# A hybrid decoder layer on one core: places of the splits and norms at the feed-forwards' ends, keys turned in three places, and the third output's place in the mixer

## The chip, the cores and the metric

The kernel runs on one core of one Trainium2 chip. The core has TensorE (matmul, PE in the profile, with its weight loads PEld), VectorE (DVE), ScalarE (ACT), GpSimd (POOL) and SyncE (SP), each with its own queue, and 16 DMA engines. The metric is the device time of one execution in microseconds.

## The reference, cut to what matters

One decoder layer over 512 tokens of 1024 features, all in float32:

```
h = x + 1/2 * swiglu_1(rmsnorm(x))                    # d_ff 2816
z = rmsnorm(h) @ w_in                                 # columns split among two groups of heads
    attention: window 128, 8 query heads on 2 key/value heads of 64, norm of q and k, rotary, sinks
    gated linear attention: 4 heads, keys of 64, values of 128, decay per key dimension, in chunks
    gla = rmsnorm(gla) * silu(gate)
h = h + concat(attention, gla) @ w_out
h = h + 1/2 * swiglu_2(rmsnorm(h))
h = h + sigmoid(rmsnorm(h) @ ple_w_gate) * rmsnorm(p @ ple_w_proj)
```

## The kernel before

The 512 tokens are four tiles of 128. Every large product is done in three matmuls: an operand is split into a rounded part ("hi") and the rest ("lo"), and hi x hi, hi x lo and lo x hi are added up in PSUM (`mm3`). Activations come out of PSUM by a cast on ScalarE (hi) and a subtraction on VectorE (lo) in `split_psum`. Weights are loaded by SP into two raw buffers (`wraw`), and `Weights.split` casts each on ScalarE (`whi`, L140) and subtracts on VectorE (`wlo`, L141) into a ring of five slots. `W.get(key, ahead)` traces the splits up to that unit and `ahead` units beyond; `stops` bounds how far.

The program's stages follow each other: the first feed-forward, the embedding's product (`pe`), the mixer's projections with both attentions, the output projection (`wo`), the second feed-forward, and the gate's product (`pgt`).

A planner orders the instructions of each engine: it simulates the program and takes what is ready by its own costs and urgencies, so the order of the text is not the order of the queues. Two things bind it. `on_pe` puts TensorE's instructions of a step behind the last one traced, which fixes TensorE's order in the mixer. `in_order` does so for TensorE, ScalarE and VectorE, for a list of steps. SP's and POOL's queues aren't bound by either.

At the end of a feed-forward, `last_tiles` lists by hand: `pd(t, q)` (six matmuls of the last down product of tile t), `update(t)` (two additions into h on VectorE, L391), `squares(t)` (ScalarE, L307), `factor(t)` (a small addition on VectorE and a power on POOL, L299), `scaled(t)` (VectorE, L316) and `turned(t)` (eight transposes of tile t on TensorE, L202, and the casts and subtractions out of PSUM). Tiles 0 and 1 are turned in the list, tiles 2 and 3 by the code that follows: behind the second and third tile of the embedding's product, and ahead of the second and third tile of the gate's. `keep(t)` saves a tile of h to memory from SP's queue. `split_gates` splits the first unit of the gate's weights.

In the mixer one list gives TensorE's order. Its PSUM has three groups of two: `psA`, `psG` (one bank each) and `psD` (two banks each). `turn_decay` turns the decayed keys (`kd`) of three token tiles one after the other through `psG`, and ScalarE copies each out (L893). `gla_decays(li)` makes the decays of level li: two subtractions (L823, L824), an exponential (L825) and two multiplications (L826, L827) in a tile `X`. `X`, `kd` and the two score matrices `At` share a tag of four slots. `gla_level(li)` multiplies them on TensorE (`gr`), and VectorE merges the result (L854). `gla_diagonal` (`gd`) is the level of single tokens. `gla_out(c)` is the output of token tile c in a `psD` bank pair: a square on ScalarE, a sum and a scale on VectorE (L927, L928), a power on POOL, and a multiplication out of PSUM (L932) that frees the pair. `attention_out` splits the attention's half (L955, L956), `gla_mix` multiplies by the gate (L943) and turns, `out_half` is the first half of the output projection for two tiles.

Of the kernel before, what the change touches and what calls it, by code (L numbers as in the profile page):

```python
# [152 lines left out]
def hymba_kernel(tc, A, out):  # L153
# [33 lines left out]
    def psG(name):  # L187
        return psp.tile([P, 512], F32, name=name, tag="psG", bufs=2)
# [12 lines left out]
    def turn(o, x):  # L201
        last_pe[0] = nc.tensor.transpose(o, x, idn).ins  # L202

    def on_pe(f, *args):

        with tc.issue_after(last_pe[0]):
            return f(*args)
# [74 lines left out]
    add_ffn(2)  # L282
    W.stops.insert(2, len(W.units))
    for c0 in (0, 512):
        for k0 in (0, 4):
            W.add_rows("pg", A["ple_w_gate"], k0, 4, c0, 512)


    last_pow = [None]
# [31 lines left out]
        norm_scaled(t, gain, nrm, norm_factor(t, name, ss))  # L321
        return t, nrm, nT, name

    def last_tiles(pd, update, gain, nT, name, third=(), fourth=()):


        sq, rs = {}, {}

        def squares(t):
            sq[t] = norm_squares(t, name)  # L330

        def factor(t):
            rs[t] = norm_factor(t, name, sq[t][1])

        def scaled(t):
            norm_scaled(t, gain(), sq[t][0], rs[t])

        def turned(t):
            norm_transpose(t, sq[t][0], nT, name, (psA, psG))

        in_order((pd, 0, 0), (pd, 1, 0), (pd, 0, 1), (update, 0), (squares, 0), (pd, 1, 1), (update, 1), (factor, 0),
                 (squares, 1), (pd, 2, 0), (pd, 2, 1), *third, (scaled, 0), (update, 2), (factor, 1), (squares, 2),
                 (pd, 3, 0), (pd, 3, 1), (scaled, 1), *fourth, (turned, 0), (update, 3), (factor, 2), (squares, 3),
                 (scaled, 2), (turned, 1), (factor, 3), (scaled, 3))
        return turned

    def norm_transpose(t, nrm, nT, name, bank=(psG, psG)):
# [209 lines left out]
    with tc.tile_pool(name="ffn1p", bufs=1, reuse_waits="tile") as fp:  # L557
        gm = gain_tile("mix_norm")
        nTm = norm_pair(xp, "mix")
        h_d = [drp.tile([P, D], F32, name=f"h_d{t}") for t in range(NT)]  # L560

        turned = []

        def finish1(pd, update):
            turned.append(last_tiles(pd, update, lambda: gm, nTm, "mx", (), [(keep, 0), (keep, 1), (keep, 2)]))
            keep(3)

        def keep(t):
            nc.sync.dma_start(out=h_d[t], in_=h[t])

        ffn(1, nT1, fp, finish1, fp, fp, None, 2)
# [39 lines left out]
    for t in range(0, NT, 2):  # L611
        eo = mp.tile([P, 8, 256], F32, name=f"eo{t}", tag="e", bufs=2).rearrange("p (t a) c -> p t (a c)", t=2)
        for i in range(2):
            ps = psD(f"pe{t + i}")
            for c in range(2):
                gemm_ts(ps[:, c], pT, t + i, [wpe[c]])
            nc.scalar.copy(eo[:, i], ps.rearrange("p a c -> p (a c)"))
            nc.sync.dma_start(out=emb_d[t + i], in_=eo[:, i])
            if t + i in (1, 2):
                turned[0](t + i + 1)  # L620


    kall = t2("kall")
# [260 lines left out]
        nc.vector.tensor_mul(kd, kd, kF)  # L884
        Xs["k"] = kdC

    def turn_decay():
        kdC = Xs.pop("k")
        for c in range(3):
            ps = psG(f"kdt{c}")  # L890
            for a in range(2):
                turn(ps[:, a * P:(a + 1) * P], kdC[:, a * 4 + c, :])
            nc.scalar.copy(kdT[:, c], ps[:, :256].rearrange("p (a c) -> p a c", a=2))  # L893

    def gla_state(c):
        dS = psG(f"dS{c}").rearrange("p (a c) -> p a c", c=P)
# [74 lines left out]
    for f, *args in (  # L971
            (queries, 0), (turn_ranks,), (queries, 1), (turn_keys,), (log_decays, 0), (queries, 2), (log_decays, 1),
            (queries, 3), (sums, 0), (turn_queries, 0), (gla_qk, 0), (sums, 1), (turn_queries, 1), (scores, 0),
            (gla_qk, 1), (turn_queries, 2), (scores, 1), (gla_qk, 2), (turn_queries, 3), (turn_scores, 0, 0),
            (gla_qk, 3), (gla_decay,), (gla_decays, 0), (scores, 2),
            (gla_v, 0), (weighted, 0), (turn_decay,), (gla_diagonal,), (turn_scores, 1, 0), (gla_decays, 1),
            (gla_v, 1), (gla_level, 0), (gla_state, 0), (turn_scores, 1, 1), (gla_decays, 2),
            (gla_v, 2), (gla_level, 1), (weighted, 1), (gla_state, 1), (scores, 3), (gla_decays, 3),
            (gla_v, 3), (gla_level, 2), (gla_state, 2), (turn_scores, 2, 0), (gla_decays, 4),
            (gla_gate, 0), (gla_level, 3), (turn_scores, 2, 1), (gla_decays, 5),  # L980
            (gla_gate, 1), (gla_level, 4), (weighted, 2), (turn_scores, 3, 0), (gla_decays, 6),
            (gla_gate, 2, 0), (gla_level, 5), (turn_scores, 3, 1), (gla_gate, 2, 1), (gla_level, 6), (gla_scores_out,),
            (weighted, 3), (gla_gate, 3, 0), (gla_out, 0), (gla_silu, 0), (gla_out, 1), (gla_silu, 1),
            (gla_gate, 3, 1), (gla_silu, 2), (gla_silu, 3), (attention_out,), (gla_out, 2),
            (gla_mix, 0, mixT), (gla_out, 3), (gla_mix, 1, mixT), (out_half, 0, 0), (out_half, 0, 1),
            (gla_mix, 2, mixT), (out_half, 1, 0), (out_half, 1, 1),
            (gla_mix, 3, mixT)):
        on_pe(f, *args)
# [9 lines left out]
    with tc.tile_pool(name="ffn2p", bufs=1, reuse_waits="tile") as fp:  # L998
# [36 lines left out]
            g3.append(gain_tile("ple_gate_norm"))  # L1035

        nT3 = norm_pair(np_, "pg")
        def split_gates():
            W.get(("pg", 0, 0), 0)

        def finish2(pd, update):
            turned[:] = [last_tiles(pd, update, lambda: g3[0], nT3, "pg", [(split_gates,)])]

        ffn(2, nT2, fp, finish2, xp, xp, "nhi", 2, lambda: norm_transpose(*pend2[NT - 1]), embedding_norm)

# [1 line left out]
    with tc.tile_pool(name="outp", bufs=1, reuse_waits="tile") as op:  # L1047
        emb = []
        for t in range(NT):
            e = op.tile([P, D], F32, name=f"emb{t}")  # L1050
            with tc.issue_after(last_pow[0]):
                nc.gpsimd.dma_start(out=e, in_=emb_d[t])
            emb.append(e)
        for c0 in (0, 512):
            tiles = [W.get(("pg", c0, k)) for k in (0, 2, 4, 6)]
            for t in range(NT):
                if c0 == 0 and t in (1, 2):
                    turned[0](t + 1)
                parts = ((0, 256), (256, 512)) if c0 and t == NT - 1 else ((0, 512),)
                for a, b in parts:  # L1060
                    sl = slice(c0 + a, c0 + b)
                    ps = psA(f"pgt{c0}_{t}_{a}")[:, :b - a]
                    gemm_ts(ps, nT3, t, [(wh[:, :, a:b], wl[:, :, a:b]) for wh, wl in tiles])
                    sg = op.tile([P, 512], F32, name=f"sgm{c0}_{t}_{a}", tag="sgm", bufs=3)[:, :b - a]
                    nc.scalar.activation(sg, ps, AF.Sigmoid)
                    nc.vector.tensor_mul(sg, sg, emb[t][:, sl])
                    nc.vector.tensor_add(sg, sg, h[t][:, sl])
                    nc.sync.dma_start(out=out[t * P:(t + 1) * P, sl], in_=sg)
# [59 lines left out]
```

## Time and profile before

| | |
|---|---|
| median of 3 runs | 1008.62 us (1008.01 to 1010.85) |
| the profiled execution | 1008.22 us |
| its span | 1006.5 us |
| TensorE matmuls busy | 971.2 us (96%) |
| TensorE weight loads busy | 807.4 us (80%) |
| VectorE busy | 645.0 us (64%) |
| ScalarE busy | 394.5 us (39%) |
| GpSimd busy | 43.7 us (4%) |
| mean granted TensorE clock | 0.989 |
| DMA | 109.91 MB, mean 109 GB/s |

The span is the time from the first to the last instruction of the profiled execution; the device time is a little longer. Busy shares are means over the whole span. A busy TensorE can still run at half clock, which the granted clock of a stretch shows.

### The profile page before, as it was taken

Reading aid. Unit: us, or ns where it says so; the run is one execution under the profiler, and the core shown is the slowest. Engines: PE = TensorE matmul, PEld = TensorE weight load, DVE = VectorE, ACT = ScalarE, POOL = GpSimd, SP = SyncE. Lnnn points to the kernel's source line nnn. Section 1 sums busy time; section 2 is a strip of 40 time slices with the busy share of each in tenths; the row PEclk is TensorE's granted clock in tenths of the full one; section 3 lists DMA queues with packets and bytes.
Section 4 is the critical chain, followed back from the end, with each engine's and each line's share of the span. In section 5 each row is a group of like instructions: output and inputs, shape, how many; then the busy total and the mean of one; then the engine's idle time right before and its main releaser. Section 6 shows DMA issues by size and latency. Waiting matters only on the chain.

```text
span 1006.5 us, 12373 instructions
## 1 busy us (share of the span) xinstructions
PE 971.2 (96%) x5090; PEld 807.4 (80%) x5090; DVE 645.0 (64%) x811; ACT 394.5 (39%) x569; POOL 43.7 (4%) x55
## 2 busy tenths in 40 slices
PE   5999999999999989998998999999999999999898
PEld 5988888888888879876766789888888888888687
DVE  6567667576675764775766364766677675757652
ACT  5443333333333245585455243333344333332441
POOL 4000000000000010200002010000000000000010
PEclk9999999999999999999998999999999999999999
DMA  8715133141330255220213246142252523303231
GB/s 290 250 47 168 41 126 125 46 167 40 126 105 1 88 186 184 88 85 1 58 50 98 84 163 242 42 168 84 96 205 75 169 83 106 124 1 104 74 126 53
DMA packets 74235, 109.91 MB, mean 109 GB/s; under 512 B 5937, under 2 KB 55234, under 8 KB 74178
## 3 DMA queue, kind: packets, MB, share of 16 engines
q1 hardware_dynamic: 72450, 102.82, 30.4%
q0 software_dynamic: 1728, 6.29, 1.8%
q8 instruction: 40, 0.66, 0.2%
q14 instruction: 17, 0.14, 0.0%
HBM read 100.72 MB, written 8.39 MB: 108 GB/s over the span
## 4 chain that ended last, share of the span: by engine, by line
PE 88%; DVE 6%; ACT 2%; DMA 2%; issue 1%; POOL 0%; SPq 0%; ACTq 0%; POOLq 0%; DVEq 0%
PE pg L199 24%; PE pu L199 24%; PE pd L199 20%; PE pgt L199 5%; PE wo L199 4%; PE aq L199 2%; PE pe L199 1%; PE kvr L199 1%; PE gqk L199 1%; PE gv L199 1%; PE gog L199 1%; DVE mx L724 1%; DMA wraw<-in_w_out_dram 1%; DVE wlo L141 1%; DVE e L722 1%
## 5 line engine op out<-in xcount | busy, mean ns | idle before, releaser
L140 ACT CAST whi<-wraw 128x1024 fp32r<-128x1024 f32 (+1 forms) x126 | 129.9, 1039 | 187.4 <-PE pd L199 136.3
L141 DVE TENSOR_TENSOR wlo<-wraw,whi 128x1024 fp32r<-128x1024 f32 (+1 forms) x124 | 149.9, 1215 | 56.0 <-ACT whi L140 53.7
L199 PE MATMUL pg<-nlo_f,whi 128*128 128x512 f32 (+1 forms) x384 | 143.0, 373 | 0.0
L199 PE MATMUL pg<-nhi_f,whi 128*128 128x512 f32 (+1 forms) x384 | 142.6, 373 | 0.2 <-ACT nhi_f L292 0.2
L199 PE MATMUL pu<-nhi_f,wlo 128*128 128x512 f32 (+1 forms) x384 | 142.6, 372 | 0.0
L199 PE MATMUL pg<-nhi_f,wlo 128*128 128x512 f32 (+1 forms) x384 | 142.6, 372 | 0.0
L199 PE MATMUL pu<-nlo_f,whi 128*128 128x512 f32 (+1 forms) x384 | 142.6, 372 | 0.0
L199 PE MATMUL pu<-nhi_f,whi 128*128 128x512 f32 (+1 forms) x384 | 142.4, 372 | 0.0
L199 PE MATMUL pd<-whi,ahi 128*128 128x512 f32 x312 | 121.4, 389 | 0.0
L199 PE MATMUL pd<-wlo,ahi 128*128 128x512 f32 x312 | 121.4, 389 | 0.0
L199 PE MATMUL pd<-whi,alo 128*128 128x512 f32 x312 | 120.6, 389 | 0.0
L391 DVE SCALAR_TENSOR_TENSOR h<-pd,h 128x512 f32<-128x512 f32 x116 | 76.5, 686 | 29.5 <-PE pd L199 29.5
L199 PEld LDWEIGHTS pg<-nhi_f,whi 128*128 128x128 f32 x384 | 72.3, 189 | 13.2 <-ACT nhi_f L292 0.7
L199 PEld LDWEIGHTS pg<-nlo_f,whi 128*128 128x128 f32 x384 | 72.6, 189 | 12.9 <-DVE nlo_f L293 0.6
L199 PEld LDWEIGHTS pg<-nhi_f,wlo 128*128 128x128 f32 x384 | 72.5, 189 | 12.5
L199 PEld LDWEIGHTS pu<-nhi_f,wlo 128*128 128x128 f32 x384 | 72.3, 188 | 12.5
L199 PEld LDWEIGHTS pu<-nhi_f,whi 128*128 128x128 f32 x384 | 72.2, 188 | 12.5
L199 PEld LDWEIGHTS pu<-nlo_f,whi 128*128 128x128 f32 x384 | 72.4, 188 | 12.3
L140 ACT CAST whi<-draw 128x1024 fp32r<-128x1024 f32 x35 | 36.8, 1053 | 96.9 <-PE pu L199 50.9
L431 DVE TENSOR_TENSOR cb<-pu,sg 128x512 f32<-128x512 f32 x44 | 30.3, 690 | 69.2 <-PE pu L199 69.2
L140 ACT CAST whi<-wpr 128x1024 fp32r<-128x1024 f32 x35 | 36.9, 1053 | 96.2 <-PE pu L199 58.2
L199 PEld LDWEIGHTS pd<-whi,ahi 128*128 128x128 f32 x312 | 58.6, 188 | 12.2
(243 smaller groups left out, 1466.5 us busy)
## 6 DMA issues: line engine op xcount, KB each, us to landing
wraw<-in_ffn_w_gate_dram SPq DMA_DIRECT2D x22, 1024.0 KB, 5.0
wraw<-in_ffn_w_up_dram SPq DMA_DIRECT2D x22, 1024.0 KB, 5.0
wpr<-in_ffn_w_down_dram SPq DMA_DIRECT2D x10, 1024.0 KB, 5.6
draw<-in_ffn_w_down_dram SPq DMA_DIRECT2D x10, 1024.0 KB, 5.2
wraw<-in_w_in_dram SPq DMA_DIRECT2D x8, 1024.0 KB, 4.9
wraw<-in_ple_w_gate_dram SPq DMA_DIRECT2D x4, 1024.0 KB, 4.8
h<-in_x_dram SPq DMA_DIRECT2D x4, 512.0 KB, 7.0
wraw<-in_ffn_w_down_dram SPq DMA_DIRECT2D x4, 512.0 KB, 3.4
```

The lines of the kernel that those rows point to most:

```text
L140: nc.scalar.copy(hi, v)
L141: (nc.gpsimd if u < 2 and i else nc.vector).tensor_tensor(lo, v, hi.bitcast(F32), op=ALU.subtract)
L199: last_pe[0] = nc.tensor.matmul(o, lhsT=l, rhs=r, start=start, stop=stop_, **kw).ins
L391: nc.vector.scalar_tensor_tensor(hs, x, 0.5, hs, ALU.mult, ALU.add)
L431: nc.vector.tensor_mul(cb[:, half].rearrange("p a c -> p (a c)"), pu, sg)
L722: nc.vector.tensor_add(half, sc[:, :, :, :nk], amask[:, 256 - nk:].unsqueeze(1).unsqueeze(1).broadcast_to([P, 2, 2, nk]))
L724: nc.vector.reduce_max(mxt.rearrange("p (g a) -> p g a", g=2)[:, :, 2 * a:2 * a + 2], half, AX.X)
```

## The change

The gate's first 512 columns are split into weight units of two, two and four row blocks instead of four and four. `last_tiles` gets a new common part and, from its callers, a list of places for what follows the last products; tiles 2 and 3 of the first feed-forward are turned one embedding tile earlier; those of the second within the gate product, behind its first half, and that product is bound to the traced order in halves. In the mixer the three turns of the decayed keys are separate steps, copied out by VectorE, the diagonal goes ahead of them, and the fourth scores go ahead of the second state; the third output follows the second half of the fourth gate directly, ahead of the SiLUs and the attention's split, and the fourth output ahead of the first mix.

```diff
@@ -282,8 +282,8 @@
     add_ffn(2)
     W.stops.insert(2, len(W.units))
     for c0 in (0, 512):
-        for k0 in (0, 4):
-            W.add_rows("pg", A["ple_w_gate"], k0, 4, c0, 512)
+        for k0, nk in ((0, 2), (2, 2), (4, 4)) if c0 == 0 else ((0, 4), (4, 4)):
+            W.add_rows("pg", A["ple_w_gate"], k0, nk, c0, 512)
 
 
     last_pow = [None]
@@ -321,7 +321,7 @@
         norm_scaled(t, gain, nrm, norm_factor(t, name, ss))
         return t, nrm, nT, name
 
-    def last_tiles(pd, update, gain, nT, name, third=(), fourth=()):
+    def last_tiles(pd, update, gain, nT, name, places):
 
 
         sq, rs = {}, {}
@@ -338,10 +338,10 @@
         def turned(t):
             norm_transpose(t, sq[t][0], nT, name, (psA, psG))
 
-        in_order((pd, 0, 0), (pd, 1, 0), (pd, 0, 1), (update, 0), (squares, 0), (pd, 1, 1), (update, 1), (factor, 0),
-                 (squares, 1), (pd, 2, 0), (pd, 2, 1), *third, (scaled, 0), (update, 2), (factor, 1), (squares, 2),
-                 (pd, 3, 0), (pd, 3, 1), (scaled, 1), *fourth, (turned, 0), (update, 3), (factor, 2), (squares, 3),
-                 (scaled, 2), (turned, 1), (factor, 3), (scaled, 3))
+        named = {"pd": pd, "update": update, "squares": squares, "factor": factor, "scaled": scaled, "turned": turned}
+        in_order((pd, 0, 0), (pd, 1, 0), (pd, 0, 1), (update, 0), (squares, 0), (pd, 1, 1), (update, 1), (squares, 1),
+                 (factor, 0), (pd, 2, 0), (pd, 2, 1), (scaled, 0), (factor, 1), (update, 2), (scaled, 1),
+                 (pd, 3, 0), (pd, 3, 1), *((named.get(f, f), *args) for f, *args in places))
         return turned
 
     def norm_transpose(t, nrm, nT, name, bank=(psG, psG)):
@@ -562,8 +562,10 @@
         turned = []
 
         def finish1(pd, update):
-            turned.append(last_tiles(pd, update, lambda: gm, nTm, "mx", (), [(keep, 0), (keep, 1), (keep, 2)]))
-            keep(3)
+            turned.append(last_tiles(pd, update, lambda: gm, nTm, "mx", [
+                ("update", 3), ("turned", 0), ("squares", 2), ("factor", 2), ("turned", 1), ("squares", 3),
+                (keep, 0), (keep, 1), ("scaled", 2), ("factor", 3), (keep, 2), (lambda: W.get(("kvr", 0, 0), 0),),
+                ("scaled", 3), (keep, 3)]))
 
         def keep(t):
             nc.sync.dma_start(out=h_d[t], in_=h[t])
@@ -616,8 +618,8 @@
                 gemm_ts(ps[:, c], pT, t + i, [wpe[c]])
             nc.scalar.copy(eo[:, i], ps.rearrange("p a c -> p (a c)"))
             nc.sync.dma_start(out=emb_d[t + i], in_=eo[:, i])
-            if t + i in (1, 2):
-                turned[0](t + i + 1)
+            if t + i < 2:
+                turned[0](t + i + 2)
 
 
     kall = t2("kall")
@@ -884,13 +886,12 @@
         nc.vector.tensor_mul(kd, kd, kF)
         Xs["k"] = kdC
 
-    def turn_decay():
-        kdC = Xs.pop("k")
-        for c in range(3):
-            ps = psG(f"kdt{c}")
-            for a in range(2):
-                turn(ps[:, a * P:(a + 1) * P], kdC[:, a * 4 + c, :])
-            nc.scalar.copy(kdT[:, c], ps[:, :256].rearrange("p (a c) -> p a c", a=2))
+    def turn_decay(c):
+        kdC = Xs["k"]
+        ps = psG(f"kdt{c}")
+        for a in range(2):
+            turn(ps[:, a * P:(a + 1) * P], kdC[:, a * 4 + c, :])
+        nc.vector.tensor_copy(kdT[:, c], ps[:, :256].rearrange("p (a c) -> p a c", a=2))
 
     def gla_state(c):
         dS = psG(f"dS{c}").rearrange("p (a c) -> p a c", c=P)
@@ -973,16 +974,16 @@
             (queries, 3), (sums, 0), (turn_queries, 0), (gla_qk, 0), (sums, 1), (turn_queries, 1), (scores, 0),
             (gla_qk, 1), (turn_queries, 2), (scores, 1), (gla_qk, 2), (turn_queries, 3), (turn_scores, 0, 0),
             (gla_qk, 3), (gla_decay,), (gla_decays, 0), (scores, 2),
-            (gla_v, 0), (weighted, 0), (turn_decay,), (gla_diagonal,), (turn_scores, 1, 0), (gla_decays, 1),
-            (gla_v, 1), (gla_level, 0), (gla_state, 0), (turn_scores, 1, 1), (gla_decays, 2),
-            (gla_v, 2), (gla_level, 1), (weighted, 1), (gla_state, 1), (scores, 3), (gla_decays, 3),
+            (gla_v, 0), (weighted, 0), (gla_diagonal,), (turn_decay, 0), (turn_scores, 1, 0), (gla_decays, 1),
+            (gla_v, 1), (gla_level, 0), (turn_decay, 1), (gla_state, 0), (turn_scores, 1, 1), (gla_decays, 2),
+            (gla_v, 2), (gla_level, 1), (weighted, 1), (turn_decay, 2), (scores, 3), (gla_state, 1), (gla_decays, 3),
             (gla_v, 3), (gla_level, 2), (gla_state, 2), (turn_scores, 2, 0), (gla_decays, 4),
             (gla_gate, 0), (gla_level, 3), (turn_scores, 2, 1), (gla_decays, 5),
             (gla_gate, 1), (gla_level, 4), (weighted, 2), (turn_scores, 3, 0), (gla_decays, 6),
             (gla_gate, 2, 0), (gla_level, 5), (turn_scores, 3, 1), (gla_gate, 2, 1), (gla_level, 6), (gla_scores_out,),
-            (weighted, 3), (gla_gate, 3, 0), (gla_out, 0), (gla_silu, 0), (gla_out, 1), (gla_silu, 1),
-            (gla_gate, 3, 1), (gla_silu, 2), (gla_silu, 3), (attention_out,), (gla_out, 2),
-            (gla_mix, 0, mixT), (gla_out, 3), (gla_mix, 1, mixT), (out_half, 0, 0), (out_half, 0, 1),
+            (weighted, 3), (gla_gate, 3, 0), (gla_out, 0), (gla_out, 1), (gla_gate, 3, 1), (gla_out, 2),
+            (gla_silu, 0), (gla_silu, 1), (attention_out,), (gla_out, 3), (gla_silu, 2), (gla_silu, 3),
+            (gla_mix, 0, mixT), (gla_mix, 1, mixT), (out_half, 0, 0), (out_half, 0, 1),
             (gla_mix, 2, mixT), (out_half, 1, 0), (out_half, 1, 1),
             (gla_mix, 3, mixT)):
         on_pe(f, *args)
@@ -1035,11 +1036,14 @@
             g3.append(gain_tile("ple_gate_norm"))
 
         nT3 = norm_pair(np_, "pg")
-        def split_gates():
-            W.get(("pg", 0, 0), 0)
+        def split_gates(k):
+            W.get(("pg", 0, k), 0)
 
         def finish2(pd, update):
-            turned[:] = [last_tiles(pd, update, lambda: g3[0], nT3, "pg", [(split_gates,)])]
+            split_gates(0)
+            turned[:] = [last_tiles(pd, update, lambda: g3[0], nT3, "pg", [
+                ("squares", 2), ("turned", 0), ("factor", 2), (split_gates, 2), (split_gates, 4), ("turned", 1),
+                ("scaled", 2), ("update", 3), ("squares", 3), ("factor", 3), ("scaled", 3)])]
 
         ffn(2, nT2, fp, finish2, xp, xp, "nhi", 2, lambda: norm_transpose(*pend2[NT - 1]), embedding_norm)
 
@@ -1054,13 +1058,18 @@
         for c0 in (0, 512):
             tiles = [W.get(("pg", c0, k)) for k in (0, 2, 4, 6)]
             for t in range(NT):
-                if c0 == 0 and t in (1, 2):
-                    turned[0](t + 1)
                 parts = ((0, 256), (256, 512)) if c0 and t == NT - 1 else ((0, 512),)
                 for a, b in parts:
                     sl = slice(c0 + a, c0 + b)
                     ps = psA(f"pgt{c0}_{t}_{a}")[:, :b - a]
-                    gemm_ts(ps, nT3, t, [(wh[:, :, a:b], wl[:, :, a:b]) for wh, wl in tiles])
+                    wt = [(wh[:, :, a:b], wl[:, :, a:b]) for wh, wl in tiles]
+                    if c0 == 0:
+                        on_pe(gemm_ts, ps, nT3, t, wt[:2], False)
+                        if t in (1, 2):
+                            on_pe(turned[0], t + 1)
+                        on_pe(gemm_ts, ps, nT3, t, wt[2:], True, 4)
+                    else:
+                        gemm_ts(ps, nT3, t, wt)
                     sg = op.tile([P, 512], F32, name=f"sgm{c0}_{t}_{a}", tag="sgm", bufs=3)[:, :b - a]
                     nc.scalar.activation(sg, ps, AF.Sigmoid)
                     nc.vector.tensor_mul(sg, sg, emb[t][:, sl])
```

## Rows read from the trace of the kernel before

**Rows 1.** The page: busy time (share of the span) and instructions of an engine.
```profile
PE 971.2 (96%) x5090; PEld 807.4 (80%) x5090; DVE 645.0 (64%) x811; ACT 394.5 (39%) x569; POOL 43.7 (4%) x55
```
**Rows 2.** TensorE's waits: line, for what, total us, times, longest us.
```profile
PE kdt L202 <- ACT kdT L893: 3.9, 1, 3.9
PE o L199 <- DVE on L932: 3.7, 2, 3.5
PE ntr_pg L202 <- ACT whi L140: 3.7, 1, 3.7
PE pe L199 <- DVE h L391: 2.5, 1, 2.5
...
PE ntr_pg L202 <- DVE nrm_pg L316: 1.0, 1, 1.0
```
**Rows 3.** Windows: length, busy PE, PEld, DVE, ACT, POOL, granted clock, DMA, GB/s.
```profile
370.40:373.80 3.40, 3.40 (x10) 2.63 (x9) 2.67 (x5) 0.67 (x2) 1.25 (x4) 0.50 0.57 227
373.80:465.90 92.10, 86.57 (x476) 71.33 (x474) 59.97 (x99) 55.88 (x122) 10.50 (x8) 1.00 0.31 103
466.00:469.40 3.40, 3.40 (x71) 2.95 (x72) 2.49 (x4) 2.95 (x7) 0.00 (x0) 0.50 0.00 0
506.90:510.30 3.40, 3.40 (x10) 2.63 (x9) 3.40 (x5) 1.92 (x5) 0.00 (x0) 0.50 0.00 0
544.50:551.30 6.80, 6.80 (x26) 5.42 (x27) 4.30 (x9) 1.19 (x2) 2.30 (x3) 0.50 0.00 0
954.10:957.50 3.40, 3.40 (x12) 2.92 (x11) 3.02 (x6) 2.06 (x6) 1.37 (x1) 0.50 0.79 301
```
**Rows 4.** Timeline of TensorE, 368 to 380: start, us, what [idle before <- releaser].
```profile
369.14 0.50 PE L199 MATMUL pe<-whi,pTwhi 128*128 128x512 f32 x1 [2.51 <-DVE h L391]
...
376.36 1.91 PE L202 MATMUL ntr_mx<-idn,nrm_mx 128*128 128x128 f32 x16
```
**Rows 5.** Timeline of VectorE, 363 to 371.
```profile
365.34 1.35 DVE L141 TENSOR_TENSOR wlo<-wraw,whi 128x544 fp32r<-128x544 f32 x2
366.61 1.28 DVE L293 TENSOR_TENSOR nlo_mix<-ntr_mx,nhi_mix 128x512 fp32r<-128x512 f32 x2
367.81 1.28 DVE L391 SCALAR_TENSOR_TENSOR h<-pd,h 128x512 f32<-128x512 f32 x2
```
**Rows 6.** The chain that ended last, in the mixer: start, us, what.
```profile
466.62 1.92 PE gd L199 x64
...
478.13 5.47 PE gv L199 x24
```
**Rows 7.** Timeline of ScalarE, 461 to 470.
```profile
465.52 0.62 ACT L893 COPY kdT<-kdt 128x256 f32<-128x256 f32 x2
```
**Rows 8.** Timeline of VectorE, 460 to 512: decays, and copies of the first state.
```profile
476.57 0.69 DVE L823 TENSOR_TENSOR X<-bT 128x512 f32<-128x512 f32 x1 [4.40 <-PE gr L199]
...
477.78 0.48 DVE L905 COPY S<-dS 128x128 f32<-128x128 f32 x2
...
479.91 0.68 DVE L827 TENSOR_TENSOR X<-X,gqT 128x512 f32<-128x512 f32 x1
...
498.91 0.68 DVE L823 TENSOR_TENSOR X<-bT 128x512 f32<-128x512 f32 x1
...
508.03 0.69 DVE L827 TENSOR_TENSOR X<-X,gqT 128x512 f32<-128x512 f32 x1
```
**Rows 9.** Timeline of VectorE, 538 to 547.
```profile
540.19 1.89 DVE L956 TENSOR_TENSOR nlo_mo<-araw,nhi_mo 128x512 fp32r<-128x512 f32 x3
...
543.65 0.69 DVE L932 TENSOR_TENSOR on<-o,rs_o 128x512 f32<-128x512 f32 x1 [0.30 <-POOL rs_o L299]
```
**Rows 10.** Timeline of VectorE, 944 to 958.
```profile
949.98 2.35 DVE L141 TENSOR_TENSOR wlo<-wraw,whi 128x1024 fp32r<-128x1024 f32 x2
952.25 1.28 DVE L316 SCALAR_TENSOR_TENSOR nrm_pg<-h,rs_pg,gain_ple_gate_norm 128x1024 f32<-128x1024 f32 x1
```
**Rows 11.** DMA issues: out<-in, queue, count, KB each, median us to landing.
```profile
wraw<-in_ple_w_gate_dram SPq DMA_DIRECT2D x4, 1024.0 KB, 4.8
```

## The prediction

> **What bounds the kernel now.** I read the page first, then TensorE's own waits, then the granted clock, and at last the order of the instructions round the few places that these two point to. The page shows the kernel bound by TensorE: its matmuls are busy for 971.2 of 1006.5 us [rows 1]. So only what TensorE loses counts, and that is little: some 35 us in the whole span, part of it at the start. The list of its waits names single places [rows 2]: 2.5 us ahead of the embedding's product at the end of the first feed-forward, 3.9 us in the transposes of the decayed keys, 3.7 us at the outputs, and 1.0 and 3.7 us in the transposes at the end of the second feed-forward. The stretches of rows 3 are what follows such a wait: the granted clock is 0.50, the 1.2 GHz level, for 3.4 us, once for 6.8 us, and 1.00 (2.4 GHz) for the 92 us between the first and the second of them. An engine busy throughout at half clock does in 3.4 us the work of 1.7, so each stretch costs up to 1.7 us on top of the wait ahead of it. The change touches four of the five stretches of rows 3; the one at 506.9 it leaves alone.
>
> **Base.** The profiled execution took 1008.2 us, 1.7 around its span of 1006.5; the median of the runs is 0.4 above it. I subtract from 1008.2.
>
> **1. End of the first feed-forward.** The embedding's product waits for tile 3's residual update, which frees the PSUM banks it will use: idle 2.51 us until 369.14 [rows 4]. On VectorE that update starts at 367.81, though its product was done at about 364.5 (an estimate: 369.14 less the 2.51 us and less some 2 us for the 16 transposes ahead, which take 1.91 us elsewhere in rows 4). Ahead of it on VectorE went two key-weight subtractions of 1.35 us together, which the planner had pulled in from later code, and a pair of 1.28 us for the first transposes [rows 5]. The new list puts the update first, so it ends near 366.0, before the transposes of tiles 0 and 1 do. The wait goes (2.5), and with it the half clock that follows (up to 1.7). What is late next is tile 2's norm: VectorE now does update, two pairs of subtractions and the scaling, four pieces of 1.28 us [rows 5] from 364.7, with some 0.6 us of waits on ScalarE, so it is ready at about 370.5. Tile 2's transposes are now traced behind the first embedding tile instead of the second, that is at 364.5 + 1.9 + 2.7 (half of a 24-matmul product, 5.47 us [rows 6]) = 369.1. The cost is 0 if the planner lets the second tile pass, 1.4 if it doesn't; I take 0.6, since before it swapped such transposes with products too. Term 1: 2.5 + 1.7 - 0.6 = **3.6**, ends 2.8 and 4.2; a loss is out, since nothing new is put ahead of the embedding's product.
> Other queues: the four saves of h on SP move behind the squares; they are read only after the mixer. The key weights' split moves some 5 us later, and with it the next load into its raw buffer; that weight is multiplied more than 20 us later, behind the embedding and the keys, and without that cover the load would cost up to the 5 us.
>
> **2. Keys in three places.** The third transpose of the decayed keys waits 3.9 us for the first copy, which ScalarE does at 465.52, behind the exponentials of the third score block [rows 2, 7]. TensorE then runs at 1.2 GHz from 466.0 to 469.4 [rows 3]. In the new order the diagonal (1.92 us in that stretch [rows 6]) comes first, and the copies stand in VectorE's queue. The trace has no copy of 128x256 from PSUM on VectorE; it lies between the 128x128 pair, 0.48 us for two, and 0.68 us for a 128x512 operation [rows 8]. I take 0.4, by the copy: 1.2 us in all, on an engine that is idle for four microseconds at that time while it waits for the same exponentials. If the first copy were queued behind them instead, the state that reads it is still a 5.5 us product away. Hence 3.9 + 1.7 = 5.6, less 0.3 for handovers of the banks among three separate turns: term 2 is **5.3**, ends 0 (the wait comes back at another bank of that pair) and 5.6.
> The price is hidden in a buffer. The decayed keys share four slots with two score matrices and the decays of the levels. Today all three turns are done before the first level; the second level's decays take the keys' slot. Now the slot is held until the third turn, behind the second level, so the second level's decays can only start when the first level has been read. Such a chain (two subtractions, exponential, two multiplies) runs from 476.57 to 480.59, 4.0 us, when nothing intervenes [rows 8]; TensorE has about 7 us between two levels (a product of 5.47 us, eight transposes, a state). So it is covered, with 3 us to spare; rival C is about the case that it isn't.
>
> **3. Third output moved.** The fourth output waits 3.5 us [rows 2] for the bank of the second, whose normalised copy VectorE finishes only at 544.34; the scale for it is queued behind three subtractions of the attention's half, 1.89 us from 540.19 [rows 9]. The half clock of 6.8 us follows. In the new text the third output is traced ahead of the attention's split and of the SiLUs. TensorE's order changes only in one respect: the fourth output no longer has the first mix's four transposes (about 0.5 us by rows 4) ahead of it. Bounds: everything goes, 3.5 + 3.4 = 6.9; or the copy is as late as now, and 0.5 us of transposes and a little more stand behind it, -0.7. I go by the row in question: the three subtractions lose their place (1.9), one of the two halves of the slow stretch goes (1.7), the transposes are behind (0.5): **3.1**.
>
> **4. End of the second feed-forward.** TensorE waits 1.0 and 3.7 us for the scaled tiles 0 and 1 [rows 2]. Both are behind weight subtractions on VectorE: two of them, 2.35 us, stand directly ahead of the scaling at 952.25 [rows 10], and an equal pair ahead of the first. In the new order one half-size unit is split ahead of everything, the scalings come without splits in front, and the other two units follow behind tile 0's transposes. 4.7 us of waits go, and the slow stretch after them: 6.4. What is late next are those three subtractions, 3.5 us, against a product that is now cut in halves and needs one unit each 1.4 us; I count 0.4 for it, and 3.5 at the worst. The third unit's load can start only when the first unit is split, and takes 4.8 us [rows 11]; the split stands ahead of the last 48 products, about twice 5.47 us [rows 6], and the load fits under them. The fourth tile's update falls behind the splits; its transposes come two and a half products later. The four embedding loads on POOL stay behind the last power, which moves by a microsecond or so; nothing on TensorE waits for them while three output buffers suffice. Term 4: **6.0**, ends 2.9 and 6.4.
>
> Both ends keep 16 transposes in a row. Such a row of 16, 1.91 us, lies inside the 92 us at 1.00 [rows 3, 4]: that many did not slow the clock there.
> The Trainium skill (TensorE: Matmul & The Clock Gate, Part 4: PE-mode transpose) says that transposes don't count as activity for the clock as matmuls do. By that rule both ends could fall to 1.2 GHz without any wait, since each still has 16 transposes in a row. The trace doesn't bear that out for this length.
>
> **Sum.** 3.6 + 5.3 + 3.1 + 6.0 = 18.0. The planner re-sorts what the lists don't state, and waits of a few microseconds are what it leaves today [rows 2]; for one more of the size of the 2.5 us one I take off 2.0. 1008.2 - 16.0 = **992.2**.
>
> **Rivals.**
> A. The mixer gives nothing: banks and slots that were late are late one step further on. For it: both mixer waits of rows 2 are on a bank, not on data, and the fourth output still needs the second's bank. Against: the copies that were late stand behind work on ScalarE that they now avoid. 1008.2 - 3.6 - 6.0 + 2.0 = 1000.6.
> B. The waits go but the clock still falls at both ends, by the transposes: 992.2 + 3.4 = 995.6. Against it: the row of 92 us. It is what the Trainium skill's rule above would do here.
> C. Slower. Place: levels two to five of the mixer. With the keys' slot held, each level's decays start only when the level before has been read. The chain can last long: 498.91 to 508.72, 9.8 us, where ScalarE stood on a weight load in between [rows 8]. Against 7 us of cover that is 2.8 us of wait and 1.7 of clock for each level, 18.0 for four; with the mixer's terms lost: 1008.2 - 9.6 + 18.0 = 1016.6. It decides when the chain exceeds 7 us and the extra slot does not come back after the third turn. Against it: it does come back there, by the text.
> D. No change: the planner answers the stated places with as many new waits: 1008.
> E. All terms at their best ends and no new wait: 1008.2 - 23.1 = 985.1.
>
> **How the numbers follow.** A difference of 0.3% (3 us) is what a measurement tells from none. Chances: forecast (988 to 997) 0.45, A 0.18, B 0.08, C 0.12, D 0.09, E 0.08. The range from 985 to 1002 takes in all but C and D, 0.79. Faster 0.79, same 0.09, slower 0.12.
>
> **What would show it.** In the changed profile: no wait of the embedding's product on the update of h, and a granted clock of 1.00 there; no wait of the key transposes on a copy; the fourth output's wait under 2 us; gate products starting within half a microsecond of the second pair of transposes at the end, and four 3.4 us pieces of half clock fewer in all. Wrong would be: waits of a level on its decays, of a key turn on a bank, or of the first gate product on a weight subtraction, and slow stretches in new places.

## The result: 993.9 us, and where it came from

The changed kernel takes 993.93 us (median of 4 runs, 992.87 to 996.07) against 1008.32 us for the kernel before, a ratio of 0.9859 with a 95% interval of 0.9831 to 0.9887. Run again later it took 993.36 us against 1006.41, 0.9872 (0.9852 to 0.9892). The forecast was 992.2, in a range of 985 to 1002; the gain is 14.4 us by the first pair of medians and 13.1 by the second, where 16.0 were forecast.

The profiled execution took 994.27 us, its span is 992.5, and the mean granted clock is 0.995 instead of 0.989. The page of the changed kernel shows 4.4 us less busy time on TensorE than [rows 1], for the same number of matmuls:

```profile
PE 966.8 (97%) x5090; PEld 804.3 (81%) x5090; DVE 646.5 (65%) x814; ACT 393.6 (40%) x566; POOL 43.3 (4%) x55
```

Its waits of TensorE (columns as in [rows 2]): the keys' turns, the embedding's product and the gate's transposes are gone from the list, and the outputs' wait has grown from 3.7 to 4.5 us.

```profile
PE o L199 <- DVE on L933: 4.5, 2, 4.4
PE pt L202 <- ACT pb L753: 2.7, 2, 2.3
...
PE ntr_mx L202 <- DVE nrm_mx L316: 0.4, 1, 0.4
```

Windows of the changed kernel, with the columns of [rows 3]: the first end, the keys, the third score block, the outputs, the second end. The clock is 1.00 at both ends and at the keys; two stretches at 0.50 are left ahead of the tail, where there were five.

```profile
364.00:378.00 14.00, 13.63 (x83) 11.82 (x82) 11.15 (x17) 9.46 (x20) 3.49 (x6) 1.00 0.53 199
458.00:472.00 14.00, 14.00 (x160) 11.65 (x150) 7.81 (x15) 9.64 (x27) 0.00 (x0) 1.00 0.00 1
497.71:501.12 3.41, 3.41 (x13) 2.84 (x11) 3.02 (x5) 0.93 (x3) 0.00 (x0) 0.50 0.02 5
...
535.25:542.07 6.82, 6.20 (x26) 5.24 (x27) 4.67 (x9) 1.65 (x3) 1.70 (x2) 0.50 0.00 1
936.00:960.00 24.00, 23.83 (x120) 19.31 (x118) 19.52 (x27) 13.24 (x23) 4.75 (x7) 1.00 0.50 186
```

The whole gain can be laid out by TensorE's own instructions. A stage here runs from the start of one named matmul to the start of another, so work that has moved within a stage doesn't matter: **end 1** from the last `pd` of the first feed-forward to the first `aq`; **keys** from the first `gv` to the last; **scores** from there to the first `o`; **outputs** from there to the first `pg`; **end 2** from the last `pd` to the last `pgt`. The times are worked out from the timelines.

| profiled execution | end 1 | keys | scores | outputs | end 2 | median, us | ratio to before (95%) |
|---|---|---|---|---|---|---|---|
| before | 31.30 | 40.03 | 37.64 | 66.69 | 54.72 | 1008.3 | |
| changed | 27.67 | 34.25 | 38.00 | 66.87 | 48.76 | 993.9 | 0.9859 (0.9831–0.9887) |
| changed, run again | 27.58 | 34.25 | 36.45 | 66.28 | 49.09 | 993.4 | 0.9872 (0.9852–0.9892) |
| 1 first end undone | 29.68 | 34.25 | 36.41 | 67.09 | 49.17 | 995.6 | 0.9900 (0.9877–0.9923) |
| 2 second end undone | 27.67 | 34.25 | 36.51 | 66.56 | 55.87 | 999.9 | 0.9927 (0.9916–0.9939) |
| 3 keys undone | 27.67 | 40.61 | 35.84 | 66.77 | 48.85 | 998.6 | 0.9920 (0.9907–0.9933) |
| 4 outputs undone | 27.67 | 34.26 | 36.33 | 66.28 | 48.97 | 993.1 | 0.9864 (0.9851–0.9877) |
| 5 subtractions behind | 27.57 | 34.25 | 37.96 | 63.83 | 49.04 | 991.2 | 0.9846 (0.9828–0.9863) |
| 6 weight split behind too | 27.58 | 34.26 | 37.66 | 61.45 | 48.65 | 988.5 | 0.9824 (0.9804–0.9843) |
| 7 as 6, old output order | 27.58 | 34.25 | 40.51 | 61.53 | 49.00 | 988.0 | 0.9819 (0.9798–0.9841) |
| 8 places alone | 27.68 | 34.26 | 37.61 | 67.15 | 48.67 | 994.6 | 0.9877 (0.9862–0.9893) |
| 9 VectorE copies alone | 27.67 | 34.50 | 35.80 | 66.50 | 49.38 | 992.0 | 0.9853 (0.9839–0.9866) |
| 10 score copy moved | 27.58 | 34.25 | 37.51 | 67.31 | 48.70 | 994.3 | 0.9876 (0.9862–0.9889) |
| 11 as 6 and 10 | 27.58 | 34.26 | 37.49 | 61.54 | 48.80 | 986.9 | 0.9808 (0.9792–0.9823) |

Before against changed: -3.63, -5.78, +0.36, +0.18, -5.96, and 0.03 between the stages, -14.80 together. A start 0.39 us later and a tail 0.46 us longer bring it to the 13.95 us by which the two executions differ. So three of the four terms came in at their size, and the outputs gave nothing.

One reserve belongs to the table's first line. The profiled execution of the kernel before has a mean granted clock of 0.989; of the 29 executions of it that were timed beside the experiments 20 have 0.991 and take 1005.6 to 1007.2 us. A stretch of 3.41 us at 0.50 lowers the mean by 0.0017, so by this estimate most executions have one such stretch less than the profile, and the usual gain is smaller by up to 1.7 us.

### The profile page after: what moved, and what is told of

Its sections match the earlier page's. It is cut to its first block, busy times and chain, and to the rows that moved or that the text cites. A ratio compares the mean times of both kernels' runs of the same rounds, so it can differ in the third digit from the quotient of the medians.

```text
span 992.5 us, 12376 instructions
## 1 busy us (share of the span) xinstructions
PE 966.8 (97%) x5090; PEld 804.3 (81%) x5090; DVE 646.5 (65%) x814; ACT 393.6 (40%) x566; POOL 43.3 (4%) x55
## 4 chain that ended last, share of the span: by engine, by line
PE 89%; DVE 5%; DMA 2%; ACT 2%; issue 1%; POOL 0%; SPq 0%; ACTq 0%; DVEq 0%; POOLq 0%
PE pg L199 24%; PE pu L199 24%; PE pd L199 21%; PE wo L199 4%; PE pgt L199 3%; PE aq L199 2%; PE gv L199 2%; PE kvr L199 1%; PE gqk L199 1%; PE gog L199 1%; DVE wlo L141 1%; DMA wraw<-in_w_out_dram 1%; PE ntr_f L202 1%; DMA h<-in_x_dram 1%; DVE e L724 1%
```

## The experiments

**1 to 4: one part undone at a time.** The theory was that the parts add; 4 asks whether the moved output is worth its 3.1 us. Line numbers of an experiment differ from the changed kernel's by the lines that its edit adds.

1, the first end back in its old order, tiles 2 and 3 turned one embedding tile later again (the cut shows the call alone):

```diff
-    turned.append(last_tiles(pd, update, lambda: gm, nTm, "mx", [("update", 3), ("turned", 0), ...
+    turned.append(last_tiles_old(pd, update, lambda: gm, nTm, "mx", (), [(keep, 0), (keep, 1), (keep, 2)]))
```

> The changed kernel with the end of the first feed-forward alone put back to its old order. Theory (the four parts act one by one, and each is worth what the start times of the same instructions differ by in the two traces): the token-embedding products start 3.6 us later again and everything behind them moves with it, so about 997.5 us against 993.9; TensorE's wait for the transposed tile at that end comes back with its half-clock stretch. Rival (the parts lean on one another: what this end gained is taken back by a later wait on VectorE or on a weight): less than 1.5 us slower than the changed kernel.

Measured: 995.64 us. The stage is 2.0 us longer, not 3.6. TensorE's timeline has the wait back at its old length, but the window around it shows a clock of 1.00, where [rows 3] has 0.50 behind the same 2.51 us:

```profile
369.83 0.50 PE L199 MATMUL pe<-whi,pTwhi 128*128 128x512 f32 x1 [2.51 <-DVE h L414]
```
```profile
365.00:377.00 12.00, 9.43 (x57) 7.86 (x56) 8.68 (x13) 6.67 (x13) 3.09 (x6) 1.00 0.59 214
```

So 2.0 us of this term are the wait, and the other 1.6 are the clock, which that wait need not cost. The total lies between the theory's 997.5 and the rival's bound of 1.5 us.

2, the second end back in its old order, with the gate's units and the bound halves:

```diff
-    for k0, nk in ((0, 2), (2, 2), (4, 4)) if c0 == 0 else ((0, 4), (4, 4)):
+    for k0 in (0, 4):
...
-    turned[:] = [last_tiles(pd, update, lambda: g3[0], nT3, "pg", [("squares", 2), ("turned", 0), ...
+    turned[:] = [last_tiles_old(pd, update, lambda: g3[0], nT3, "pg", [(split_gates,)])]
```

> The changed kernel with the end of the second feed-forward alone put back, with the gate's halves as they were. Theory: 6.0 us slower, about 999.9 us; the old wait of the first transposes there (3.6 us in the kernel before) is back, and a half-clock stretch of 3.41 us beside it. Rival (the gain there came from the start being earlier, not from the order): under 3 us slower.

Measured: 999.85 us. The stage is 6.8 to 7.1 us longer. Both waits of [rows 2] are back, and here the half clock behind them (0.74 over 13 us) lasts 6.8 us instead of 3.4:

```profile
939.42 1.06 PE L202 MATMUL ntr_pg<-idn,nrm_pg 128*128 128x128 f32 x8 [1.03 <-DVE nrm_pg L316]
944.15 1.94 PE L202 MATMUL ntr_pg<-idn,nrm_pg 128*128 128x128 f32 x8 [3.67 <-DVE nrm_pg L316]
```
```profile
939.00:952.00 13.00, 8.91 (x35) 7.47 (x36) 11.83 (x18) 6.91 (x14) 4.06 (x5) 0.74 0.47 162
```

3, the keys' turns back in one place, with copies on ScalarE, and the diagonal and the fourth scores back at their old places (the cut shows the first line of the list):

```diff
-    nc.vector.tensor_copy(kdT[:, c], ...)
+    nc.scalar.copy(kdT[:, c], ...)
...
-    (weighted, 0), (gla_diagonal,), (turn_decay, 0), (turn_scores, 1, 0)
+    (weighted, 0), (turn_decay, 0), (turn_decay, 1), (turn_decay, 2), (gla_diagonal,), (turn_scores, 1, 0)
```

> The changed kernel with the transposed keys back in one place, one after another, with copies on ScalarE. Theory: 5.8 us slower, about 999.7 us, with the waits of the transposes for the copies and the half-clock stretch back. Rival (the gain there came from the state's and the scores' order): below 2 us slower, with the wait moved elsewhere.

Measured: 998.62 us, the stage 6.4 us longer, with the third turn waiting as in [rows 2]. The score block behind it is 0.6 us shorter than in the changed kernel's second profile, so a little is given back there.

```profile
462.84 0.69 PE L202 MATMUL kdt<-idn,kd 128*128 128x128 f32 x2 [3.85 <-ACT kdT L894]
```

4, the mixer's tail in its old order:

```diff
-    (gla_out, 0), (gla_out, 1), (gla_gate, 3, 1), (gla_out, 2), (gla_silu, 0), ..., (gla_out, 3), ...
+    (gla_out, 0), (gla_silu, 0), (gla_out, 1), ..., (attention_out,), (gla_out, 2), (gla_mix, 0, mixT), (gla_out, 3), ...
```

> The changed kernel with the tail of the mixer in its old order (third output late, the gates' sigmoid products between the outputs). Theory from the traces (moving the third output removed no wait, because VectorE still has three subtractions of the attention's mix ahead of the norm that the outputs wait for): -1 to +0.5 us, so 993 to 994.5 us, with the half-clock stretch of 6.83 us there in either order. Rival, the prediction's step: 3.1 us slower, 997 us.

Measured: 993.1 us, the outputs' stage 66.28 us, that of the changed kernel's second profile. The move is worth nothing. By the medians 1 to 3 cost 2, 6 and 5 us (for 1 the interval overlaps with that of the changed kernel's second measurement). By the stages they cost 2.0, 7.1 and 6.4, together 15.5, where the same stages gained 15.4: the parts add, though single ones differ by up to 1.6 us with the clock.

**Why the outputs gave nothing.** In the changed kernel the fourth output still waits for the multiplication that empties the second output's bank pair. VectorE's timeline answers [rows 9]: the same three subtractions, 1.89 us, still stand ahead of the small scale (L929) that the multiplication (L933) needs. They follow `attention_out` in the text, which now comes after the third output, yet the planner put them where they were.

```profile
531.56 1.89 DVE L957 TENSOR_TENSOR nlo_mo<-araw,nhi_mo 128x512 fp32r<-128x512 f32 x3
533.37 0.16 DVE L929 TENSOR_SCALAR oss<-oss 128x4 f32<-128x4 f32 x1
...
535.03 0.69 DVE L933 TENSOR_TENSOR on<-o,rs_o 128x512 f32<-128x512 f32 x1 [0.90 <-POOL rs_o L299]
```

ScalarE's timeline shows a second cause, which I had not seen, though it stands in the trace of before too. In the changed kernel the second output is out at about 526.1, but its square runs at 528.88, behind a cast of the output weight that waits 2.12 us for a gate product to give back a ring slot.

```profile
527.82 1.15 ACT L137 ACTIVATE whi<-wraw,c_gla_out_norm 128x1024 fp32r<-128x1024 f32 x1 [2.12 <-PE gog L199]
528.88 0.58 ACT L926 ACTIVATE osq<-o 128x512 f32<-128x512 f32 x1
```

The same cast in the kernel before, with the same wait:

```profile
536.45 1.15 ACT L137 ACTIVATE whi<-wraw,c_gla_out_norm 128x1024 fp32r<-128x1024 f32 x1 [2.12 <-PE gog L199]
```

5, the subtractions alone queued behind the second output's multiplication:

```diff
-    nc.vector.tensor_sub(mixT[1][:, 0:4, tokens(t)], araw[:, :, tokens(t)], ...)
+    with tc.issue_after(on_ins[1]):
+        nc.vector.tensor_sub(mixT[1][:, 0:4, tokens(t)], araw[:, :, tokens(t)], ...)
```

> The changed kernel, and the four subtractions of the attention's half queued on VectorE behind the normalised copy of the second output, which is what the prediction took the moved third output to do. Theory (moving the third output in the text left these subtractions where they were, and they are what was mis-sized): the fourth output's wait falls from 4.35 to about 2.3 us, since the copy starts 1.9 us earlier; with up to 1.7 us of half clock gone, -2 to -3.7 us, so 990 to 992 us. Rival (the wait is set by the square on ScalarE, which comes late behind the weight casts): the wait stays over 3.5 us, time within 1 us of the changed kernel.

Measured: 991.17 us, 2.2 below the changed kernel beside it (993.36), and each of its four runs (at most 992.14) is faster than each of the changed kernel's eight (at least 992.87), though the intervals of the two ratios overlap. The fourth output waits 2.24 us instead of 4.35, the clock there is half for 3.4 us instead of 6.8, and the outputs' stage is 2.5 to 3.0 us shorter. That is close to the 3.1 us of the prediction, for the edit that does what the prediction ascribed to the other. TensorE's timeline:

```profile
533.41 0.68 PE L199 MATMUL o<-gv,At 128*128 128x128 f32 x4 [2.24 <-DVE on L933]
```

6, also the split of that output weight behind the second output's square and gated copy:

```diff
+    def gated(c):
+        mul_ins[c] = nc.vector.tensor_mul(ons[c], ons[c], gog[c]).ins
+    def split_out():
+        with tc.issue_after(sq_ins[1]), tc.issue_after(mul_ins[1]):
+            W.get(("wo", 0, 4), 0)
...
-    (gla_out, 0), (gla_out, 1), (gla_gate, 3, 1), (gla_out, 2), (gla_silu, 0), (gla_silu, 1),
+    (gla_out, 0), (gla_out, 1), (gla_silu, 0), (gla_silu, 1), (gated, 0), (gated, 1),
+    (split_out,), (gla_gate, 3, 1), (gla_out, 2),
```

The subtractions now follow `mul_ins[1]`, and `W.get` of the value and gate weights looks less far ahead, so that the split isn't made early.

> As the one before, and also the split of the second output-weight unit queued behind the square of the second output on ScalarE and behind that output's gated copy on VectorE, with the gating of the first two outputs ahead of both. Theory (two things hold the second output's bank: a weight cast on ScalarE that waits 2.12 us for a gate product, and the subtractions on VectorE): the copy is ready at about 531.7 instead of 535.7, the fourth output's wait falls to 0 to 0.8 us, the half clock there goes or halves, -4 to -7 us, so 987 to 990 us. Rival (the output product only waits elsewhere, for its weights or for the attention's low halves): less than 2 us better than the kernel before this one, with a new wait of the output product of over 2 us.

Measured: 988.47 us, the stage 61.45. The square runs at 525.83, the multiplication at 530.11 instead of 535.03, and the wait is 0.20 us. Of ScalarE, VectorE and TensorE, in that order:

```profile
525.83 0.60 ACT L926 ACTIVATE osq<-o 128x512 f32<-128x512 f32 x1 [1.34 <-PE o L199]
```
```profile
530.11 0.69 DVE L933 TENSOR_TENSOR on<-o,rs_o 128x512 f32<-128x512 f32 x1 [1.19 <-POOL rs_o L299]
```
```profile
530.86 0.71 PE L199 MATMUL o<-gv,At 128*128 128x128 f32 x4 [0.20 <-DVE on L933]
```

And the windows over the outputs, of the changed kernel, of 5 and of 6: the clock goes from 0.84 by 0.92 to 1.00, and TensorE's busy time in these 22 us from 17.47 to 20.52.

```profile
523.00:545.00 22.00, 17.47 (x93) 14.05 (x92) 15.62 (x25) 9.74 (x16) 6.47 (x8) 0.84 0.40 117
```
```profile
523.00:545.00 22.00, 19.59 (x110) 15.51 (x109) 15.44 (x26) 9.84 (x16) 6.16 (x8) 0.92 0.40 115
```
```profile
523.00:545.00 22.00, 20.52 (x118) 15.95 (x117) 15.86 (x26) 9.90 (x16) 6.16 (x8) 1.00 0.40 115
```

6 moves more than the one split: two casts of output weights, the gating and the SiLUs of the first two outputs, and the splits of the weights ahead. The trace shows the square freed from the cast; how the 2.4 us that the stage gains over 5 divide among these moves is not shown.

7, as 6 with the outputs in the old order of 4:

> As the one before, with the old order of the outputs in the mixer's tail (third output behind the gates' last half and the attention's split, fourth behind the first mix's transposes). Theory (the third output's place is worth nothing by itself, since TensorE runs it at the same moment in both orders): within 1 us of the kernel before this one. Rival (its place pays once the copy of the second output is early): 2 us or more slower than the kernel before this one.

Measured: 988.03 us and 61.53 us of outputs: the order is worth nothing here either. Its profiled execution, 991.28 us, was 3 us above its median; ScalarE's cast there waited 2.36 us for a weight load (0.87 in the changed kernel's first profile, 0.58 in its second), and the third score block's transposes waited 3.78.

```profile
495.73 1.04 ACT L140 CAST whi<-wraw 128x1024 fp32r<-128x1024 f32 x1 [2.36 <-DMA wraw<-in_w_out_dram]
```

**8 and 9: which half of the keys' change does it.** 8 keeps the three places and puts the copies back on ScalarE; 9 keeps VectorE's copies and puts the turns back in one place. Each is one half of the diff of 3.

> The changed kernel with its three places for the transposed keys, but with the copies back on ScalarE. Theory (the places alone carry the keys' gain: with a turn between other work the banks are not wanted at once): no wait of a key turn over 0.5 us, and from the first value product to the end of the last as long as in the changed kernel, 34.2 us, not 40; the wait of the third score block's transposes can become shorter, since its copy moves on ScalarE too, so -3 to +0.5 us against the changed kernel, 990 to 994 us. Rival (the copies on VectorE carry it): the first copy waits on ScalarE behind the exponentials and a state or a key turn waits 2 us or more, +2 to +5 us.

> The changed kernel with the keys' three turns back in one place, one after another, but with the copies on VectorE. Theory (either half suffices: VectorE is idle when the first turn ends, so the third turn waits for a copy of 0.4 us and its handover only): a wait of 0.3 to 1.2 us, no half clock, 0 to +1.5 us against the changed kernel, 993.5 to 995 us. Rival (the place carries it): 2 us or more of wait and a half-clock stretch, +3 us or more.

Measured: the stage is 34.26 and 34.50 us. Either half is enough. 8 has no wait of a key turn in its list; in 9 the turns run almost together. TensorE's timeline of 9:

```profile
458.69 0.66 PE L202 MATMUL kdt<-idn,kd 128*128 128x128 f32 x4 [0.32 <-ACT araw L765]
```

The times differ from those expected by what the score blocks do: in 8 the third block's wait has gone over to the fourth (2.50 us, with a half clock behind it), so the 3 us that I allowed as a gain did not come; in 9 the wait is 1.70 us with no half clock.

**10 and 11: the wait at the third score block.**

```diff
-    (nc.scalar.copy if kb == 0 else nc.vector.tensor_copy)(pb, pt)
+    (nc.scalar.copy if kb == 0 and n != 2 else nc.vector.tensor_copy)(pb, pt)
```

> The changed kernel with the first copy of the third score block's transposes on VectorE instead of ScalarE, where it stands behind an exponential and a weight cast. Theory (that copy's queue is what remains of the wait at 497 us): the wait of 2.0 to 2.3 us falls below 0.5 us and no half clock follows, -2 to -4 us, 990 to 992 us. Rival (VectorE has its own work there, the decays of a level behind which the next level waits): the wait moves to a level and less than 1 us is won.

Measured: 994.25 us, so the theory fell. The wait at 497 is gone, but TensorE is then early for the fourth block, whose copy stands on ScalarE behind a table load and two SiLUs. It waits there 2.31 us, with a half-clock stretch of 3.4 us. Neither the expected gain nor the rival's place came true. ScalarE and TensorE of 10:

```profile
507.97 1.28 ACT L940 ACT_TABLE_LOAD   x1
509.27 1.15 ACT L940 ACTIVATE gog<-gog 128x512 f32<-128x512 f32 x2
510.32 0.99 ACT L753 COPY pb<-pt 128x1024 f32<-128x1024 f32 x1
```
```profile
511.37 1.97 PE L202 MATMUL pt<-idn,e 128*128 128x128 f32 x8 [2.31 <-ACT pb L753]
```

> The kernel with the second output's copy early (the one that had the split of the output weights behind the square of the second output, and the new place of the third output), together with the copy of the third score block on VectorE. Theory (the two are 30 us apart on TensorE and add): 2 to 4 us below that kernel's 988.5, so 985 to 987 us. Rival (they don't add, since the second hangs on the order of VectorE's queue that the first has changed): 988 us or more.

Measured: 986.86 us, ratio 0.9808 (0.9792 to 0.9823), faster than before and, by intervals that don't overlap, than the changed kernel. That it is 1.6 us faster than 6 is not shown: the scores' stage is 37.49 against 37.66 us, and the intervals overlap. What it gains stands in 6.

The changed kernel itself was run again beside 5 to 7:

> The changed kernel once more, unaltered, as the measure for the kernels beside it: 992.5 to 995 us, ratio to the kernel before 0.984 to 0.988. The half-clock stretch near 497 us may be there or not, since it was there in one profile of this order and not in another of nearly the same (the one with the old tail); if it is not, the span is up to 1.7 us shorter.

Measured: 993.36 us; its second profile has a wait of 2.00 us at the score block and no half clock, and a stage 1.55 us shorter.

## Why the prediction was right, and where it wasn't

**Term 1 (3.6): 3.63, in part by luck.** The 2.5 us of wait less what came late next were read rightly. The other 1.6 are a half-clock stretch that the profile of before had and that the same wait did not bring in 1. In the changed kernel VectorE's update ends at 366.19 (forecast: near 366.0), the embedding's product starts right behind the 16 transposes, tile 2's norm ends at 370.79 (about 370.5), and the planner let the second embedding tile pass ahead of tile 2's transposes. What is late next is 0.37 us, at tile 3, where I had taken 0.6. TensorE, to hold against [rows 4]:

```profile
364.63 0.39 PE L199 MATMUL pd<-whi,alo 128*128 128x512 f32 x1
364.86 1.91 PE L202 MATMUL ntr_mx<-idn,nrm_mx 128*128 128x128 f32 x16
366.52 0.48 PE L199 MATMUL pe<-whi,pTwhi 128*128 128x512 f32 x1
...
373.47 1.06 PE L202 MATMUL ntr_mx<-idn,nrm_mx 128*128 128x128 f32 x8 [0.37 <-DVE nrm_mx L316]
```

**Term 2 (5.3): 5.78.** The copy on VectorE, which no row of before showed, takes 0.41 us (taken: 0.4). The hidden price was read rightly too. VectorE starts the second level's decays only when the first level has been read, and is done at 471.1; TensorE wants them at 474.03. That leaves 2.9 us of the 3 forecast, and rival C did not come to decide.

```profile
460.13 0.41 DVE L894 COPY kdT<-kdt 128x256 f32<-128x256 f32 x1
...
466.70 0.69 DVE L825 TENSOR_TENSOR X<-bT 128x512 f32<-128x512 f32 x1 [2.57 <-PE gr L199]
...
470.41 0.68 DVE L829 TENSOR_TENSOR X<-X,gqT 128x512 f32<-128x512 f32 x1
```

What I could not tell apart is that either half of that edit would have done (8, 9).

**Term 3 (3.1): -0.2 by the traces, 0 by 4 and 7.** The step that failed is "the three subtractions lose their place". I read the queue off the order of the text, though a planner sorts VectorE's queue, as the section on the kernel says. Their price was right: 5 takes their place away and gets 2.5 to 3.0 us. The transposes ahead of the fourth output cost nothing either, since it was waiting for longer than they take.

**Term 4 (6.0): 5.96.** The gate's product starts directly behind the transposes, and the three subtractions of 3.50 us on VectorE run beside its first matmuls. TensorE and VectorE of the changed kernel, the latter against [rows 10]:

```profile
939.31 1.91 PE L202 MATMUL ntr_pg<-idn,nrm_pg 128*128 128x128 f32 x16
941.30 0.50 PE L199 MATMUL pgt<-whi,nhi_pg 128*128 128x512 f32 x1
```
```profile
941.99 3.50 DVE L141 TENSOR_TENSOR wlo<-wraw,whi 128x1024 fp32r<-128x1024 f32 x3
```

**The reserve (-2.0).** Of the new waits that it stood for, 0.3 us came (the third score block, from 1.99 to 2.29). So the sum was near in part by luck: what the outputs fell short by, 3.3 us, was met by 1.7 us of the reserve that did not come and by 0.5 us more from the keys. The later start and the longer tail, 0.85 us together, stood in no term.

Rival A was right about the outputs, whose wait stayed on the bank, and wrong about the keys. Rival B did not come: both ends have 16 transposes in a row at a clock of 1.00. The Trainium skill (TensorE: Matmul & The Clock Gate, Part 4: PE-mode transpose) would let the clock fall there; no run here shows it for 1.91 us of them. Of the four half-clock pieces that were to go, three went; the outputs' 6.8 us stayed, were halved by 5 and went with 6.

## What to carry to other kernels

Where a planner orders an engine's queue, a step moved in the text is a request, not an order: price it at zero until an edge binds the instructions that make the waiter late, and follow the waiter's whole chain (here ScalarE's square as well as VectorE's subtractions) before choosing which. A wait on a PSUM bank is ended by the engine that empties it, so the copy on an idle engine and the turn at a later place were here two cures for the same thing, and one was enough (8, 9). Removing one wait on a queue that several steps share can hand it to the next step of that queue, as 10 shows; look for the next waiter before counting the gain.

## What the runs showed of the hardware

The clock behind a wait is less certain than I took it to be. Over the fourteen profiles TensorE had 15 waits of 1.70 to 2.51 us at the places spoken of here; nine came with a 3.4 us stretch at 0.50 (1.2 GHz), begun in the last 0.5 us of the wait or within 1.5 us behind it, and six with none, also for the same wait in the same place: 2.51 us at the first end cost a stretch before and none in 1, and 1.99 and 2.00 us at the score block had one in 6 and none in the second profile of the changed kernel. A wait of 1.69 us ahead of the output projection, in every one of the profiles, came with none. All waits of 3.5 us and more there had a stretch, begun during the wait or just behind it, of 3.4 us in two cases and of 6.8 us in the others. So a short wait is priced with 0 to 1.7 us of clock on top (an estimate: half of the 3.4), and differences of that size between two profiles are no sign of a cause.
